# Six entries of the table of expected waits that merges the mixers' streams on TensorE: gates, softmax attention and token-major values later

## The chip, the cores and the metric

The kernel runs on one core of a Trainium2 chip. A core has a matrix engine (TensorE, "PE" in the profile), a vector engine (VectorE, "DVE"), an engine for activation functions (ScalarE, "ACT"), a general engine (GpSimd, "POOL") and an engine that issues DMAs (SyncE, "SP"). Each works through its own list of instructions in order; an instruction waits at the head of the list until what it needs is there, and all that stands behind it waits too. The metric is the device time of one execution in microseconds, the median of several runs.

## The reference, cut to what matters

One inference step of a two-layer trunk on 512 prompt positions and 8 x 4 sample positions, so 544 columns in all. In each layer four groups of "mixers" work on slices of one projection; their outputs are joined by `w_out`, and a gated feed-forward block with a short convolution follows.

```
def hybrid_layer(x, pos, k_pos, st, p):
    h = rmsnorm(x, p['norm1_g'])
    proj = h @ p['w_in']
    (a_qkv, a_z, a_b, a_a, b_b, b_c, b_h, c_q, c_k, c_v, d_u, d_v) = jnp.split(proj, ...)
    qkv, a_conv_new = causal_dwconv(st['a_conv'], a_qkv, p['a_conv_w'])
    q, k, v = l2norm(qkv[:, :, 0]), l2norm(qkv[:, :, 1]), qkv[:, :, 2]
    beta = jax.nn.sigmoid(a_b)
    g = -jnp.exp(p['a_log']) * jax.nn.softplus(a_a + p['a_dt_bias'])
    o, a_state_new = gated_delta_rule(q, k, v, g, beta, st['a_state'])      # group A
    ...
    out_b = b_b * bx                                                        # group B
    out_c = window_attn_banded(cq, ck, cv, p['c_sinks'])                    # group C
    out_d = chunk_token_mlp(du, dvn, p['d_ws'], p['d_bias'])                # group D
    x = x + jnp.concatenate([out_a, out_b, out_c, out_d], axis=-1) @ p['w_out']
    h2 = rmsnorm(x, p['norm2_g'])
    gate, f_conv_new = causal_dwconv(st['f_conv'], h2 @ p['ffn_w_gate'], p['ffn_conv_w'])
    return x + (jax.nn.silu(gate) * (h2 @ p['ffn_w_up'])) @ p['ffn_w_down'], new
```

## The kernel before, in words

Activations lie feature-major (128 features on the partitions, 544 positions along the free dimension). Each float32 product is made of three float32r products: high by high, high by low, low by high. So each weight tile is split in two: ScalarE copies the high part (`wh`, L734), VectorE subtracts it to get the low part (`wl`, L736).

In each layer a **main stream** (`main`) issues the large products in a fixed order: first the token-major projection (`ptm`), then 19 tiles of 128 output features (`pj_...`), of which the first nine are k0, q0, v0, cq0, cq1, ck, k1, q1, v1, then the output projection (`po1`, `po2`) and the feed-forward block (`pgt`, `pup`, `pA` to `pD`, `pdn`). A tile `pj_...` takes eight *steps*; a step is one slice of the contraction, 6 matmuls (two halves of 272 columns, three products each). Two PSUM buffers (`psmm`, pool `pmm`) hold the tiles in turn, so tile n+2 can begin only when VectorE has read tile n out. For k, q and v that reading is L1529 and L1530, for cq and ck it is L1550.

Beside it run **side streams**, one for each mixer and layer, written as Python generators:

- `gates` (g0 in layer 0, g1 in layer 1): the products `pg`, a chain of small VectorE instructions that ends in `gg` (L867), then the products `pe` on `gg`, read by `gcp` (L882) and `ex`.
- `mixer_a` (a00, a01, a10, a11: layer and pair of heads): norms (`pl`), decays (`pgb`, from `gg`), `pk` (k by k and k by q, in two halves that use the same PSUM buffer `pk`, so the second half waits until VectorE has read the first: `N` L967, `qk` L968), then `pkt`, k turned token-major, which VectorE makes into `kbe` and `kd` (L1006, L1008), then `pvt`, v turned token-major, in the same PSUM buffer as `pkt`, then a triangular inverse (`pW`, `pR`) and a scan (`p`).
- `decode_a` (e0, e1), `mix_d` (d0, d1), and `mix_c` (c0, c1): softmax attention in four blocks of scores (`psc`), transposes (`ptr`) and values (`pov`). The scores need `cq` and `ck` after their rotation, whose last VectorE instruction is L1555.

A class `Order` merges these streams into the one list of TensorE. It keeps a clock of its own in model microseconds, moved on by a price for each matmul. A stream yields either a delay or the name of an event; the table `LAT` adds, for a stream's n-th yield, a further delay. A side stream is taken as soon as its model time has come, otherwise the main stream goes on. TensorE's list is fixed in this way; the lists of the other engines are then made by a scheduler that works from the same program. The lines that use the table:

```
        w = LAT.get(st[3], {}).get(st[4], 0.0)
        if isinstance(y, tuple):
            st[0], st[2] = self.t, (y[1], w)
        else:
            st[0], st[2] = self.t + y + w, None
```

In `gates` the second yield is `yield 9.0`, between the chain to `gg` and the products `pe`. In `mix_c` the first is the wait for the event `c0` or `c1`, set 4.0 model us after the tile ck is issued. In `mixer_a` the twelfth is `yield 1.8`, between `pkt` and `pvt`.

Of the kernel before, what the change touches and what calls it, by code (L numbers as in the profile page):

```python
# [273 lines left out]
def _unhost(r):  # L274
# [8 lines left out]
    def conv(a, k, n):  # L283
# [19 lines left out]

LAT = {
    "a00": {
        3: 1.60, 13: 15.62, 14: 3.75, 15: 2.87, 16: 1.87, 17: 3.23, 18: 1.78, 19: 2.03, 34: 1.52,
    },
    "a01": {
        3: 3.96, 4: 1.12, 10: 2.64, 24: 0.84,
    },  # L310
    "a10": {
        3: 1.56, 13: 15.67, 14: 3.68, 15: 2.79, 16: 3.85, 17: 1.45, 25: 1.33, 36: 0.47, 42: 1.13,
    },
    "a11": {
        3: 3.59, 6: 3.32, 13: 1.06, 28: 0.70, 35: 0.30,
    },
    "c0": {
        1: 1.19, 2: 4.34, 5: 7.17, 6: 0.65, 7: 2.67, 8: 3.40,
    },
    "c1": {  # L320
        1: 0.81, 2: 4.06, 5: 7.68, 6: 0.61, 7: 15.38, 10: 1.48,
    },
    "d0": {
        4: 6.53,
# [5 lines left out]
        4: 3.69,  # L330
    },
    "g0": {
        2: 2.70,
    },
    "g1": {
        2: 2.53,
    },
}

# [1488 lines left out]
```

## Time and profile before

| | us |
|---|---|
| median of 3 runs | 1355.7 |
| lowest and highest run | 1353.25, 1356.69 |
| the profiled execution | 1355.9 |
| its span, first to last instruction | 1353.6 |
| TensorE busy | 1297.3 |
| VectorE busy | 994.2 |
| ScalarE busy | 638.2 |
| GpSimd busy | 459.6 |

The mixers of layer 0 take about the stretch from 35 to 260 us of the span, those of layer 1 from 699 to 925. A row of the timeline gives the start, the duration, the engine, the line, the operation, output and inputs, the count of instructions merged in the row, and in brackets the idle time of the engine just before with the instruction that ended it. All TensorE products have line L436 or L441, so they are told apart by their output. A row of the stretches gives from and to, the length, the busy time of TensorE, its weight loads, VectorE, ScalarE and GpSimd (with counts), TensorE's granted clock (1.00 is 2.4 GHz, 0.50 is 1.2 GHz), and two columns on DMA.

### The profile page before, as it was taken

How to read it: one execution, taken by the hardware profiler on the slowest of the kernel's cores; microseconds unless marked ns; L12 is line 12 of the kernel's file. 1: busy time of each engine (PE TensorE's matmuls, PEld its weight loads, DVE VectorE, ACT ScalarE, POOL GpSimd, SP SyncE). 2: the span in 40 equal slices, each digit the busy share in tenths (PEclk: the TensorE clock that was granted, in tenths of full speed). 3: DMA queues.
4: the chain of work that ended last, by engine and by line, in shares of the span. 5: the costliest groups of instructions: out<-in, count | busy, mean ns of one | idle time of the engine just before them, and what ended most of it. 6: DMA issues, size and time to landing. Idle time of an engine off the chain costs nothing.

```text
span 1353.6 us, 29982 instructions
## 1 busy us (share of the span) xinstructions
PE 1297.3 (96%) x12550; PEld 1247.8 (92%) x12550; DVE 994.2 (73%) x1579; ACT 638.2 (47%) x1116; POOL 459.6 (34%) x570
## 2 busy tenths in 40 slices
PE   9899999997999999999998999999979999999997
PEld 8888888996999999999998888889979999999997
DVE  6898944669689778777558977547697896886865
ACT  6436323454455445444434363335545554454453
POOL 2432320043365544542123322102334454643501
PEclk9899999997999999999998999999979999999999
DMA  7222241231233332333432221413212333232231
GB/s 277 82 66 81 79 131 42 87 100 33 79 99 96 104 93 87 104 93 103 157 104 81 77 84 53 137 40 95 98 31 79 110 98 91 94 108 87 87 100 67
DMA packets 48087, 125.61 MB, mean 93 GB/s; under 512 B 10144, under 2 KB 14432, under 8 KB 47824
## 3 DMA queue, kind: packets, MB, share of 16 engines
q1 hardware_dynamic: 47952, 123.70, 29.2%
q8 instruction: 98, 1.61, 0.5%
q14 instruction: 37, 0.30, 0.1%
HBM read 115.01 MB, written 8.67 MB: 91 GB/s over the span
## 4 chain that ended last, share of the span: by engine, by line
PE 79%; DVE 14%; ACT 3%; issue 3%; DMA 1%; DVEq 0%; SPq 0%; ACTq 0%
PE pdn L436 16%; PE pA L436 11%; PE pD L436 7%; PE po L436 7%; PE pB L436 4%; PE pup L436 4%; DVE wl L736 3%; PE pC L436 3%; PE pgt L436 3%; PE ptm L436 2%; PE pj_b L436 2%; PE pj_cq L436 2%; PE pj_z L436 2%; PE pj_h L436 2%; PE pj_c L436 2%
## 5 line engine op out<-in xcount | busy, mean ns | idle before, releaser
L736 DVE TENSOR_TENSOR wl<-wr,wh 128x768 fp32r<-128x768 f32 (+3 forms) x218 | 267.5, 1227 | 68.8 <-ACT wh L734 67.4
L734 ACT ACTIVATE wh<-wr 128x768 fp32r<-128x768 f32 (+3 forms) x218 | 193.1, 886 | 186.9 <-PE pA L436 32.8
L436 PE MATMUL pdn<-hdh,wh 128*128 128x272 f32 x680 | 141.5, 289 | 5.9 <-DVE up L1743 4.1
L436 PE MATMUL pdn<-hdl,wh 128*128 128x272 f32 x680 | 140.7, 288 | 0.5 <-DVE hdl L516 0.5
L436 PE MATMUL pdn<-hdh,wl 128*128 128x272 f32 x680 | 140.5, 288 | 0.0
L717 POOL TENSOR_TENSOR s<-wr 128x512 f32<-128x512 f32 x36 | 53.5, 1487 | 229.9 <-DMA wr<-w_u 140.8
L734 ACT ACTIVATE wh<-s 128x1024 fp32r<-128x1024 f32 x72 | 76.2, 1059 | 93.8 <-PE pdn L436 69.3
L436 PEld LDWEIGHTS pdn<-hdh,wh 128*128 128x128 f32 x680 | 106.5, 188 | 8.1 <-issue 3.9
L436 PEld LDWEIGHTS pdn<-hdl,wh 128*128 128x128 f32 x680 | 106.6, 188 | 0.9 <-DVE hdl L516 0.9
L736 DVE TENSOR_TENSOR wl<-s,wh 128x1024 fp32r<-128x1024 f32 x72 | 101.8, 1414 | 7.1 <-ACT wh L734 7.0
L436 PEld LDWEIGHTS pdn<-hdh,wl 128*128 128x128 f32 x680 | 106.5, 188 | 0.0
L798 DVE SCALAR_TENSOR_TENSOR cacc<-pbf,prm,cacc 128x560 f32<-128x560 f32 x88 | 78.6, 894 | 34.8 <-ACT cacc L796 34.0
L536 POOL TENSOR_TENSOR sq<-sq 128x544 f32<-128x544 f32 x18 | 30.8, 1715 | 201.3 <-DVE xl L562 135.3
L1769 DVE TENSOR_TENSOR xr<-xr,pdn 128x544 f32<-128x544 f32 x62 | 44.3, 715 | 47.2 <-PE pdn L436 47.1
L1669 POOL COPY sfo<-pbf 128x2 f32<-128x2 f32 x44 | 20.8, 472 | 136.7 <-DVE pbf L1734 84.0
L718 POOL TENSOR_TENSOR s<-wr,s 128x512 f32<-128x512 f32 x36 | 65.3, 1813 | 1.3
L720 POOL TENSOR_TENSOR s<-wr 128x512 f32<-128x512 f32 x36 | 62.1, 1725 | 0.0
L719 POOL TENSOR_TENSOR s<-wr,s 128x512 f32<-128x512 f32 x36 | 59.2, 1645 | 5.7 <-DVE wl L736 4.9
L796 ACT ACTIVATE cacc<-pbf,prm 128x560 f32<-128x560 f32 x44 | 33.6, 764 | 53.8 <-DVE pbf L1735 51.7
L516 DVE TENSOR_TENSOR hdl<-sl,hdh 128x544 fp32r<-128x544 f32 x44 | 41.3, 939 | 1.9 <-ACT hdh L515 1.8
L436 PE MATMUL pA<-f5h,wh 128*128 128x272 f32 x144 | 41.7, 289 | 0.0
L436 PE MATMUL pB<-f3h,wl 128*128 128x272 f32 x144 | 41.6, 289 | 0.0
(635 smaller groups left out, 4227.3 us busy)
## 6 DMA issues: line engine op xcount, KB each, us to landing
wr<-w_g SPq DMA_DIRECT2D x44, 512.0 KB
wr<-w_u SPq DMA_DIRECT2D x44, 512.0 KB
wr<-w_ch SPq DMA_DIRECT2D x38, 512.0 KB
wr<-w_d SPq DMA_DIRECT2D x48, 384.0 KB
wr<-w_o SPq DMA_DIRECT2D x12, 384.0 KB
wr<-w_d SPq DMA_DIRECT2D x16, 256.0 KB
xr<-x_in SPq DMA_DIRECT2D x7, 544.0 KB
wr<-w_tm SPq DMA_DIRECT2D x8, 392.0 KB
```

What stands on the lines that cost most here:

```text
L436: nc.tensor.matmul(out, lhsT, rhs, **kw)
L516: tt(lo, src, hi.bitcast(F32), op=ALU.subtract)
L536: (dve if self.last is not None else self.es[i]).tensor_tensor(self.acc[i], self.acc[i], sq, op=ALU.add)
L717: add(s12[:, lo_], u[:, lo_], u[:, hi_], op=ALU.add)
L718: add(s12[:, hi_], g[:, lo_], s12[:, lo_], op=ALU.add)
L719: add(s43[:, lo_], g[:, hi_], s12[:, hi_], op=ALU.add)
L720: add(s43[:, hi_], g[:, lo_], u[:, lo_], op=ALU.add)
L734: act(hi, r, AF.Copy)
L736: tt(lo, r, hi.bitcast(F32), op=ALU.subtract)
L796: act(acc[:, 0:out_n], pb[:, 0:out_n], AF.Copy, scale=wcol[:, 0:1])
L798: stt(acc[:, 0:out_n], pb[:, j:j + out_n], wcol[:, j:j + 1], acc[:, 0:out_n], op0=ALU.mult, op1=ALU.add)
L1769: tt(xk(m), xk(m), pflat(p), op=ALU.add)
```

## The change

Six numbers of the table are raised or added: the second yield of `gates` from 2.70 to 7.00 and from 2.53 to 6.80; the first of `mix_c` from 1.19 to 3.60 and from 0.81 to 3.20; and the twelfth of `mixer_a`'s first pair of heads, which had no entry, to 0.90 in both layers. No arithmetic changes. Lines of the diff:

```
     "a00": {
-        3: 1.60, 13: 15.62, 14: 3.75, 15: 2.87, 16: 1.87, 17: 3.23, 18: 1.78, 19: 2.03, 34: 1.52,
+        3: 1.60, 12: 0.90, 13: 15.62, 14: 3.75, 15: 2.87, 16: 1.87, 17: 3.23, 18: 1.78, 19: 2.03, 34: 1.52,
...
     "c0": {
-        1: 1.19, 2: 4.34, 5: 7.17, 6: 0.65, 7: 2.67, 8: 3.40,
+        1: 3.60, 2: 4.34, 5: 7.17, 6: 0.65, 7: 2.67, 8: 3.40,
...
     "g0": {
-        2: 2.70,
+        2: 7.00,
```

Since a side stream's time sets where it is merged, and the merged order sets the times of all that follows, the order changes through both mixer stages. In steps of the main stream, counted from the start of each layer's tiles, the side work stands as follows (layer 0): `pe` after step 20 before and 27 now, `pde` (the decode mixer's first products) 24 and 31, the first `pl` 35 and 34, `pgb` 45 and 44, `pk` 53 and 52, its second half 54 and 54, the first `psc` 54 and 56, `pkt` 56 and 56, `pvt` 59 and 60, then most groups one to three steps later. In layer 1: `pe` 20 and 26, `pk` 53 and 52, its second half 54 and 54, the first `psc` 54 and 55, `pkt` 56 and 55, `pvt` 59 and 59; from step 90 to 144 most groups of the second pair of heads and of the decode mixer stand one to six steps earlier than before.

TensorE, layer 0, at the gates (`pj_v` is the tile v0, `pj_cq` the tile cq0, `pe` the gates' second products), before:

```order
L436 MATMUL pj_v_631<-xh,wl 128x272 x2
L436 MATMUL pe<-gg,cst 128x16 x3
L436 MATMUL pe<-gg,cst 128x1 x2
L436 MATMUL pe<-gmk,cst 128x16
L436 MATMUL pj_v_631<-xh,wh 128x272 x2
```

and now:

```order
L436 MATMUL pj_cq_704<-xh,wl 128x272 x2
L436 MATMUL pe<-gg,cst 128x16 x3
L436 MATMUL pe<-gg,cst 128x1 x2
L436 MATMUL pe<-gmk,cst 128x16
L436 MATMUL pj_cq_704<-xh,wh 128x272 x2
```

The gates' products have moved from the middle of tile v0 to behind the third step of tile cq0.

TensorE, layer 0, at the first scores (a piece of the difference; `pj_k` is the tile k1, the `pk` row its second half, the first being two steps ahead):

```order
 L436 MATMUL pj_k_976<-xl,wh 128x272 x2
 L436 MATMUL pj_k_976<-xh,wl 128x272 x2
-L436 MATMUL psc<-ck,cq 128x128 x4
+L436 MATMUL pj_k_976<-xh,wh 128x272 x2
+L436 MATMUL pj_k_976<-xl,wh 128x272 x2
+L436 MATMUL pj_k_976<-xh,wl 128x272 x2
 L436 MATMUL pk<-kq_439 64x128 x8
 L436 MATMUL pj_k_976<-xh,wh 128x272 x2
```

The scores have left the place ahead of the second half of `pk`, and that half now comes two steps after the first with no scores between. VectorE's list at the same place, before:

```order
L736 TENSOR_TENSOR wl<-wr,wh 128x1024
L1553 TENSOR_TENSOR ck<-rp,rope 128x544
L1555 TENSOR_TENSOR ck<-ck,rs 128x544
L967 TENSOR_TENSOR N<-pk,N 128x256
L968 TENSOR_TENSOR qk<-pk,qk 128x256
```

and now:

```order
L1553 TENSOR_TENSOR ck<-rp,rope 128x544
L967 TENSOR_TENSOR N<-pk,N 128x256
L968 TENSOR_TENSOR qk<-pk,qk 128x256
L1555 TENSOR_TENSOR ck<-ck,rs 128x544
L967 TENSOR_TENSOR N<-pk,N 128x256
```

The reading of the first half of `pk` has moved ahead of the last instruction on `ck`.

VectorE, layer 1, at the token-major keys (`kbe`, `kd` from `pkt`; `pb` is the reading of tile k1, `wl` a weight split), before:

```order
L972 STREAM_TRANSPOSE NT<-N 128x512
L1240 TENSOR_SCALAR nm<-mx 128x4
L1529 TENSOR_TENSOR pb<-pj_k_9243,rstd 128x512
L1530 TENSOR_TENSOR pb<-pj_k_9243,rstd 128x8x4
L1242 TENSOR_TENSOR es<-prm_120,nm 128x4
L976 COPY_PREDICATED R<-cst,NT 128x256
L736 TENSOR_TENSOR wl<-wr,wh 128x1024
L1006 TENSOR_TENSOR kbe<-pkt,bec 128x512
L976 COPY_PREDICATED R<-cst,NT 128x256
L1008 TENSOR_TENSOR kd<-pkt,ex 128x512
```

and now:

```order
L972 STREAM_TRANSPOSE NT<-N 128x512
L1237 TENSOR_REDUCE mx<-sc 128x2
L1006 TENSOR_TENSOR kbe<-pkt,bec 128x512
L1008 TENSOR_TENSOR kd<-pkt,ex 128x512
L976 COPY_PREDICATED R<-cst,NT 128x256
L1238 TENSOR_TENSOR mx<-mx,prm_120 128x4
L1529 TENSOR_TENSOR pb<-pj_k_9243,rstd 128x512
L1530 TENSOR_TENSOR pb<-pj_k_9243,rstd 128x8x4
L736 TENSOR_TENSOR wl<-wr,wh 128x1024
```

`kbe` and `kd` have moved ahead of the reading of tile k1 and of a weight split.

## Rows read from the trace of the kernel before

**Rows 1.** The page: busy times, and the chain that ended last, by engine.

```profile
PE 1297.3 (96%) x12550; PEld 1247.8 (92%) x12550; DVE 994.2 (73%) x1579; ACT 638.2 (47%) x1116; POOL 459.6 (34%) x570
PE 79%; DVE 14%; ACT 3%; issue 3%; DMA 1%; DVEq 0%; SPq 0%; ACTq 0%
```

**Rows 2.** What TensorE waited for: total us, times, longest us.

```profile
PE pgt L436 <- DVE f1l L587: 16.1, 6, 6.0
PE pe L436 <- DVE gg L867: 8.7, 2, 4.3
PE psc L436 <- DVE ck L1555: 4.2, 2, 2.1
...
PE pvt L436 <- DVE kd L1008: 1.1, 2, 0.6
```

**Rows 3.** Stretches at the gates: length, busy PE PEld DVE ACT POOL, granted clock.

```profile
47.60:50.10 2.50, 0.00 (x1) 0.00 (x0) 2.47 (x8) 0.42 (x1) 0.36 (x1) 1.00 0.18 66
50.10:60.40 10.30, 8.46 (x39) 8.46 (x39) 6.76 (x18) 5.55 (x11) 2.60 (x6) 0.50 0.15 52
...
715.70:726.00 10.30, 8.69 (x40) 8.69 (x40) 6.67 (x18) 5.33 (x9) 2.60 (x6) 0.50 0.15 52
```

**Rows 4.** Timeline of TensorE, layer 0: start, duration, instruction, idle before.

```profile
44.42 0.41 PE L436 MATMUL pj_v<-xh,wh 128*128 128x272 f32 x2
...
47.19 0.41 PE L436 MATMUL pj_v<-xh,wl 128*128 128x272 f32 x2
51.94 2.29 PE L436 MATMUL pe<-gg,cst 128*128 128x16 f32 x10 [4.34 <-DVE gg L867]
...
54.52 0.80 PE L436 MATMUL pj_v<-xh,wh 128*128 128x272 f32 x2
...
60.83 0.50 PE L436 MATMUL pj_cq<-xh,wh 128*128 128x272 f32 x2
...
88.59 0.72 PE L436 MATMUL psc<-ck,cq 64*128 64x128 f32 x8 [2.10 <-DVE ck L1555]
...
96.23 1.15 PE L436 MATMUL pvt<-cst,vt 64*64 64x64 f32 x32 [0.54 <-DVE kd L1008]
```

**Rows 5.** Timeline of VectorE, layer 0.

```profile
51.38 0.18 DVE L1530 TENSOR_TENSOR pb<-pj_q,rstd 128x32 f32<-128x32 f32 x1
...
60.35 0.69 DVE L1529 TENSOR_TENSOR pb<-pj_v,rstd 128x512 f32<-128x512 f32 x1 [3.42 <-PE pj_v L436]
...
86.94 1.60 DVE L1555 TENSOR_TENSOR ck<-ck,rs 128x544 f32<-128x544 f32 x1
...
88.80 0.41 DVE L968 TENSOR_TENSOR qk<-pk,qk 128x256 f32<-128x256 f32 x1
...
95.41 0.68 DVE L1008 TENSOR_TENSOR kd<-pkt,ex 128x512 f32<-128x512 f32 x1
```

**Rows 6.** Stretches from the changed VectorE order to `qk` and `kd`.

```profile
55.10:89.20 34.10, 32.00 (x241) 31.12 (x240) 28.68 (x43) 14.58 (x25) 13.89 (x12) 0.92 0.28 92
720.30:754.70 34.40, 32.29 (x242) 31.37 (x241) 28.70 (x43) 14.58 (x25) 13.81 (x12) 0.92 0.27 93
55.10:96.10 41.00, 38.46 (x319) 36.88 (x318) 35.40 (x61) 18.72 (x37) 15.56 (x16) 0.94 0.26 80
```

**Rows 7.** Timeline of TensorE, layer 1, at the same three places.

```profile
717.31 2.29 PE L436 MATMUL pe<-gg,cst 128*128 128x16 f32 x10 [4.31 <-DVE gg L867]
...
754.06 0.72 PE L436 MATMUL psc<-ck,cq 64*128 64x128 f32 x8 [2.11 <-DVE ck L1555]
...
761.70 1.15 PE L436 MATMUL pvt<-cst,vt 64*64 64x64 f32 x32 [0.55 <-DVE kd L1008]
```

**Rows 8.** Other waits of TensorE, and the clock after the first of them.

```profile
311.30 0.39 PE L436 MATMUL pgt<-f1l,wh 128*128 128x272 f32 x1 [1.71 <-DVE f1l L587]
...
788.30 0.75 PE L436 MATMUL pR<-Wc,Tm 32*32 32x32 f32 x64 [1.39 <-ACT Wc L1024]
...
313.00:330.00 17.00, 9.21 (x36) 8.29 (x36) 17.00 (x24) 7.35 (x15) 7.38 (x8) 0.50 0.00 0
```

## What was predicted

> **What bounds the kernel now.** First the page: TensorE is busy for 1297 of 1354 us and holds 79% of the chain that ended last, VectorE 14% [rows 1]. So time is won only where TensorE stands idle or runs at a lower clock. Second the list of what it waited for [rows 2]. The largest entry, 16.1 us for `f1l` at the start of the feed-forward block, is not touched. The next ones in the mixers are those of the three raised entries: `gg` 8.7, `ck` 4.2 and `kd` 1.1 us, each twice, once a layer. Third the stretches around the gates [rows 3]: TensorE does nothing from 47.6, VectorE is busy for 2.47 of the 2.50 us up to 50.1, and then the granted clock stands at 0.50 for 10.3 us, though TensorE is busy for 8.46 of them. So the wait for `gg` costs twice, once as idle time and once as half speed after it. Layer 1 repeats it with 8.69 busy us. Fourth, VectorE's own rows: between 55.1 and 89.2 it is busy for 28.68 of 34.1 us [rows 6], and its largest idle time, 3.42 us, is a wait for tile v0, which the half clock made late [rows 5]. VectorE is close to its limit there. That decides how much of the gain survives.
>
> **What the change takes away.** (1) The gates' wait. `pe` goes behind the rest of v0 and some steps of cq0, so TensorE has work while VectorE finishes `gg`. This removes 4.34 us in layer 0 [rows 4] and 4.31 in layer 1 [rows 7]. (2) The half clock after it. 8.46 and 8.69 us of work at 0.50 would take half at 1.00: 4.2 and 4.3 us [rows 3]. (3) The waits for `ck`, 2.10 and 2.11, and for `kd`, 0.54 and 0.55 [rows 4, 7]. Together 8.54 + 8.5 + 4.21 + 1.09 = 22.3 us. Nothing is added to any engine's work; the instructions are the same.
>
> **What comes late next: the buffer of tile q0.** Tile cq0 uses the PSUM buffer that q0 leaves when L1530 has read it, at 51.38 + 0.18 = 51.56 [rows 5]. A step takes 0.755 us (12 pairs start 0.252 apart, 44.42 to 47.19 [rows 4]), so v0's last four steps end at 47.60 + 3.02 = 50.6, and cq0 waits for about 0.95 us. The L1530 of layer 1 stands at the same distance from `gg`, so 1.9 us in both. The nearest rows are waits of 1.39 and 1.71 us; a clock fall follows the second and not the first [rows 8]. I take no fall.
>
> **What comes late next: the second half of `pk`.** From cq0's start to the old wait for `ck` TensorE needs 60.83 to 86.49, or 25.7 us, and now also `pe` (51.94 to 54.52 at half clock, so 1.3) and the three `pde` products, some 0.6 by the six of `pe` [rows 4]. So it comes to that half at 51.6 + 25.7 + 1.9 = 79.2. There it must wait until VectorE has read the first half (L968). VectorE's list up to L968 holds the same instructions as before except that L1555 on `ck`, 1.60 us, now comes after it. With no idle time at all it ends at 55.1 + 28.68 - 1.60 = 82.2 [rows 5, 6]. So TensorE waits for 3.0 us at a place where it waited for `ck` for 2.1; L968's old end, 89.21, shows that this half was already as late as the scores ahead of it. In layer 1 the same sum gives 720.3 + 28.70 - 1.60 = 747.4 for VectorE; TensorE, idle from 713.0, is there the same 31.6 us later as in layer 0 (47.6 to 79.2), at about 744.6, so it waits for 2.8. The entry for the scores only lets them give their place to another reader of the same queue.
>
> **Then `kd`.** VectorE ends `kd` at 55.1 + 35.40 = 90.5 at the earliest [rows 6]. TensorE has 7.25 us of work from the second half of `pk` to `pvt` (the half itself about 1.0 and `pkt` 1.1, by the 1.15 of `pvt`; six steps 4.5; the scores 0.65), so at full clock it arrives at 89.45 and waits for about 1.1. `pvt` begins near 90.6 where it began at 96.23, and one step more of the main stream lies before it: a gain of 5.6 + 0.75 = 6.4 us. In layer 1 `kd` stands some 2.9 us earlier in VectorE's list, and there are five steps, not six, so `pvt` follows at 747.4 + 6.5 = 753.9 against 761.70: 7.8 us. From `pvt` on I carry these gains through: what follows keeps its distances or is one to three steps later in layer 0, and in the stretch after the mixers TensorE is the only busy engine. For the groups of layer 1 that come up to six steps earlier I take nothing; their bounds are the wait of 1.39 us there, which may go, and about two new ones of that size [rows 8].
>
> **Does the clock fall again?** This is the open price. A wait of 2.1 us brought no fall, 4.3 us brought one, and so did 1.71 us amid full-width products [rows 3, 4, 8]. The new wait of 3.0 us lies between, nearer to the cases that fell in kind: it is one unbroken gap, with half-filled products around it. I take a fall as the likelier. It would begin about 2.5 us into the gap, as at the gates (47.6 to 50.1), and last 10.3 us, to about 92.0. TensorE then does 4.9 of its 7.25 us of work by 92.0 and begins `pvt` at 94.35: a gain of 1.9 + 0.75 = 2.6 us. In layer 1 it lasts to 757.3, 4.95 of 6.5 us are done, and `pvt` begins at 758.9: 2.8 us. The Trainium skill, "TensorE: Matmul & The Clock Gate", section "HAM oscillation — how this bites in real kernels", says that a loop whose matrix engine waits between its bursts falls back to the half clock at every such wait, and its section "Terms" prices a fall at half of the time for which it holds. By that rule filling one gap only moves the fall to the next, and of the 8.5 us in (2) nothing would stay; the trace agrees as to the price and, by the wait of 2.1 us without a fall, not as to every wait.
>
> **The sum.** Against the profiled execution's 1355.9 us (span 1353.6 and 2.3 around it; the median is 1355.7, so nothing is shifted): 2.6 + 2.8 = 5.4 us, **1350.5 us**.
>
> **The rivals.**
> - *The new wait brings no fall.* For it: waits of 2.1 us are free of one; VectorE's instructions may be slower or faster by a microsecond. Gain 6.4 + 7.8 = 14.2: 1341.7. With a fall in one layer only, 9.2 to 10.4: about 1346.
> - *All three waits go and VectorE does not bind.* It would need VectorE to end L968 3 us sooner than its own busy time allows. Gain 22.3 - 1.9 = 20.4: 1335.5. Small chance.
> - *Nothing is won.* The fall at `pk` holds for 17 us, as after 311.3 [rows 8], and costs 3.4 us more in each layer: 5.4 - 6.8 = -1.4, so 1357.3, no change that can be told.
> - *Slower.* In layer 1 the second pair of heads and the decode mixer come one to six steps earlier, so TensorE reaches products whose inputs ScalarE or VectorE has not made; two waits of 1.7 us, each with a fall of 4.2, cost 11.8: 1350.5 + 11.8 = 1362.3. It decides from about 9.5 us of such losses. Against it: the rows show one wait of 1.39 us in that stretch, and VectorE is less busy there.
> - *The table doesn't move what it says.* Excluded: the order shows `pe` behind three steps of cq0.
>
> **How the numbers follow.** Fall in both layers 0.42, in one 0.2, in none 0.18, all waits gone 0.05, nothing won 0.09, slower 0.06. The likeliest is the first, with a range of its own from 1348.5 to 1352.5, since the unknown is where in the gap the fall begins. The range for 8 in 10 goes from 1340 to 1354.5: it leaves out the case with all waits gone, the lower part of "none", and the last two cases above. A difference of 0.3% is 4.1 us, about what a measurement of this kernel can tell from no change; the limit is 1351.6. Of the first case some seven tenths lie below it, all of the next three but a little: 0.29 + 0.19 + 0.18 + 0.05 = 0.71 faster, 0.23 within, 0.06 slower.
>
> **What would show it.** In the changed kernel's list of TensorE's waits `gg`, and `ck` ahead of `psc`, should be gone or under 0.5 us each; an entry for `pk` released by `qk` (L968) of about 3 us a layer should be new; one for `pj_cq` released by L1530, about 1 us. The stretch that held clock 0.50 at the gates should read 1.00, with a new stretch of 0.50 some 30 us later. VectorE should show almost no idle time from 55 to 90 us. I am wrong if `pk` waits for under 1.5 us, if VectorE's busy time in that stretch changes by more than 2 us, or if a new wait appears after `pvt`.

## The result, and the profile after

The changed kernel takes 1364.4 us (six runs, 1361.25 to 1368.76) where the kernel before takes 1355.5 beside it: a ratio of 1.007, with a 95% interval from 1.0049 to 1.0092. It became slower by 0.7%. The prediction was 1350.5 with a range of 1340 to 1354.5, so it is wrong in sign. The profiled execution took 1367.5 us, 3 above the median; its span is 1365.7, 12.1 more than before.

The page after, its busy times and its chain [rows 1]: TensorE's work is the same, its share of the chain fell from 79 to 74%, and what came in is "issue" and ScalarE.

```profile
PE 1300.5 (95%) x12550; PEld 1248.7 (91%) x12550; DVE 992.8 (73%) x1579; ACT 637.4 (47%) x1115; POOL 458.0 (34%) x570
PE 74%; DVE 14%; issue 5%; ACT 5%; POOL 1%; DMA 1%; SPq 0%; DVEq 0%; ACTq 0%; POOLq 0%
```

TensorE's timeline of layer 0 up to `pvt`, only rows with a wait or of the gates (it answers to [rows 4]):

```profile
51.12 0.49 PE L436 MATMUL pj_cq<-xh,wh 128*128 128x272 f32 x2 [1.09 <-DVE d L865]
53.46 1.17 PE L436 MATMUL pe<-gg,cst 128*128 128x16 f32 x10
...
62.05 0.43 PE L436 MATMUL pl<-sqd,cst 128*128 128x64 f32 x2 [1.15 <-ACT ex L884]
67.53 0.50 PE L436 MATMUL pl<-hvh,bonesr 128*128 128x512 f32 x1 [1.98 <-ACT sqd L922]
84.75 1.09 PE L436 MATMUL pk<-kq 64*64 64x128 f32 x16 [0.77 <-DVE qk L968]
93.81 1.15 PE L436 MATMUL pvt<-cst,vt 64*64 64x64 f32 x32 [1.32 <-DVE mx L1238]
```

The waits for `gg` and `ck` are gone. The first row is the wait for q0's buffer (L865 is the neighbour of L1530 in VectorE's list). Two waits are new and were not in the prediction's sum: `pl` waits for ScalarE, for `ex` and `sqd`. `pvt` starts 2.4 us earlier in the span than before, 1.8 us earlier when counted from the start of v0. The same place in layer 1, which answers to [rows 7]:

```profile
733.75 0.43 PE L436 MATMUL pl<-sqd,cst 128*128 128x64 f32 x2 [1.04 <-ACT ex L884]
739.23 0.50 PE L436 MATMUL pl<-hvh,bonesr 128*128 128x512 f32 x1 [1.97 <-ACT sqd L922]
756.43 1.09 PE L436 MATMUL pk<-kq 64*64 64x128 f32 x16 [2.26 <-DVE qk L968]
763.34 1.15 PE L436 MATMUL pvt<-cst,vt 64*64 64x64 f32 x32
```

What comes behind `pvt`, in the rows of TensorE's waits and of its timeline (layer 0 at 126.71, the rest layer 1):

```profile
126.71 1.07 PE L436 MATMUL pR<-Wc,Tm 32*32 32x32 f32 x64 [5.59 <-ACT Wc L1024]
...
793.52 1.15 PE L441 MATMUL ptr<-cst,sc 128*128 128x128 f32 x8 [2.56 <-DVE sc L1253]
803.58 0.42 PE L436 MATMUL pmd<-wm,dvd 32*64 32x32 f32 x4 [2.76 <-ACT oc L1354]
840.38 1.05 PE L441 MATMUL ptr<-cst,sc 128*128 128x128 f32 x4 [1.72 <-DVE vnd L1211]
870.16 0.32 PE L436 MATMUL pR<-Wc,Tm 32*32 32x32 f32 x14 [1.26 <-issue]
```

And the stretches with their granted clock (columns as in [rows 3]):

```profile
47.00:50.50 3.50, 3.04 (x25) 2.81 (x23) 3.47 (x9) 1.41 (x3) 1.07 (x2) 1.00 0.22 83
50.50:60.80 10.30, 9.68 (x78) 9.59 (x78) 10.11 (x20) 6.34 (x11) 4.82 (x9) 1.00 0.31 99
69.08:72.49 3.41, 3.41 (x16) 3.22 (x15) 3.41 (x6) 2.95 (x4) 0.68 (x1) 0.50 0.10 20
123.69:130.52 6.83, 3.81 (x77) 3.75 (x78) 3.70 (x12) 3.05 (x9) 0.00 (x0) 0.50 0.01 2
802.95:809.77 6.82, 6.19 (x105) 5.39 (x105) 3.65 (x7) 1.23 (x3) 1.55 (x3) 0.50 0.02 7
```

The gates run at full clock now. The half clock stands at other places, three of them behind waits: at 69 behind `pl`, at 124 in the wait of `pR`, at 803 in that of `pmd`. Two shorter ones, 3.4 us each, follow the waits at 840 and 870.

**Where the time went.** The main stream is the same in all these kernels, so the start of one and the same step can be compared. Steps are counted here through both layers: layer 1 starts with step 152. The table gives it against the kernel before, in us, set to zero at the start of v0 in layer 0; each column is one profiled execution. Side work that stands earlier or later shifts a single row by one or two us. The experiments of the other columns follow below.

| step, and its start before | after | gates alone (e1) | gates at 24 (e5) | rear kept (e6) | rear kept in layer 1 (e13) | e9 |
|---|---|---|---|---|---|---|
| 32, behind `pe` and `pde`, 66.9 | -7.1 | -7.1 | -7.1 | -7.1 | -7.1 | -6.9 |
| 48, ahead of `pk`, 80.6 | -1.9 | -1.9 | -4.6 | -1.9 | -3.5 | -4.6 |
| 60, behind `pvt`, 98.2 | -2.7 | -1.9 | -4.9 | -1.8 | -1.3 | -4.9 |
| 148, end of layer 0's mixers, 224.2 | +5.5 | -1.4 | -4.7 | +2.4 | +6.9 | -4.8 |
| 168, v0 of layer 1, 709.8 | +6.5 | -1.0 | -4.5 | +0.3 | +8.4 | -5.8 |
| 184, behind the gates, 732.4 | -0.8 | -8.2 | -9.9 | -7.0 | +1.2 | -11.3 |
| 212, behind `pvt`, 763.6 | +2.2 | -1.6 | -8.0 | -4.0 | +4.2 | -13.0 |
| 303, end of layer 1's tiles, 895.7 | +14.3 | -0.2 | -8.2 | -3.4 | +6.8 | -12.7 |

Read the first column downwards: 7.1 us won at the gates, 5.2 of them given back before `pk`, 2.7 left behind `pvt`. From there to the end of the mixers layer 0 loses 8.2. Layer 1 wins 7.3 at its gates, has 4.3 left behind `pvt`, and then loses 12.1.

### The profile page after: what moved, and what is told of

Same layout as the page of the kernel before. It is cut to its first block, busy times and chain, and to the rows that moved or that the text cites. A ratio compares the mean times of both kernels' runs of the same rounds, so it can differ in the third digit from the quotient of the medians.

```text
span 1365.7 us, 29991 instructions
## 1 busy us (share of the span) xinstructions
PE 1300.5 (95%) x12550; PEld 1248.7 (91%) x12550; DVE 992.8 (73%) x1579; ACT 637.4 (47%) x1115; POOL 458.0 (34%) x570
## 4 chain that ended last, share of the span: by engine, by line
PE 74%; DVE 14%; issue 5%; ACT 5%; POOL 1%; DMA 1%; SPq 0%; DVEq 0%; ACTq 0%; POOLq 0%
PE pdn L436 16%; PE pA L436 11%; PE pD L436 7%; PE po L436 7%; PE pB L436 4%; PE pup L436 4%; PE pgt L436 3%; PE pC L436 3%; DVE wl L736 3%; PE pj_z L436 2%; PE ptm L436 2%; PE pj_b L436 2%; DVE cacc L798 2%; PE pj_h L436 2%; PE pj_c L436 2%
## 5 line engine op out<-in xcount | busy, mean ns | idle before, releaser
L736 DVE TENSOR_TENSOR wl<-wr,wh 128x768 fp32r<-128x768 f32 (+3 forms) x218 | 272.2, 1249 | 70.8 <-ACT wh L734 69.6
L717 POOL TENSOR_TENSOR s<-wr 128x512 f32<-128x512 f32 x36 | 56.9, 1581 | 229.6 <-DMA wr<-w_u 107.3
L798 DVE SCALAR_TENSOR_TENSOR cacc<-pbf,prm,cacc 128x560 f32<-128x560 f32 x88 | 78.8, 896 | 34.4 <-ACT cacc L796 33.5
L720 POOL TENSOR_TENSOR s<-wr 128x512 f32<-128x512 f32 x36 | 62.1, 1724 | 0.0
L436 PE MATMUL pD<-f4h,wl 128*128 128x272 f32 x144 | 41.6, 289 | 0.0
```

What stands on the lines that cost most here:

```text
L436: nc.tensor.matmul(out, lhsT, rhs, **kw)
L717: add(s12[:, lo_], u[:, lo_], u[:, hi_], op=ALU.add)
L720: add(s43[:, hi_], g[:, lo_], u[:, lo_], op=ALU.add)
L736: tt(lo, r, hi.bitcast(F32), op=ALU.subtract)
L798: stt(acc[:, 0:out_n], pb[:, j:j + out_n], wcol[:, j:j + 1], acc[:, 0:out_n], op0=ALU.mult, op1=ALU.add)
```

## The experiments

Theory A: what the change wins ahead of `pvt` is real, and it is the order behind `pvt` that makes it slower. Rival B: the moves ahead of `pvt` themselves cost, through VectorE or through later falls of the clock. All ratios are against the kernel before, run beside.

**e1 to e3: one entry at a time.**

```
e1   "g0": { 2: 7.00 },  "g1": { 2: 6.80 }
e2   "c0": { 1: 3.60, ... },  "c1": { 1: 3.20, ... }
e3   "a00", "a10": { ..., 12: 0.90, ... }
```

> Only the gates' entries are raised (7.00 and 6.80); scores and values keep their old entries. TensorE's list behind pvt is then that of the kernel before, to the step. Theory A (the gates' gain is real, and the loss of the changed kernel comes from where scores and values then stand in the lists behind pvt): both waits for gg go and the half clock after them, and of the 17 us about 3 us a layer are kept up to pvt and carried on, since nothing behind pvt moves: about 1349, certainly under 1352. Rival B (VectorE and later falls of the clock take back all that the gates win, and this is why the changed kernel is slower): 1355 or more.

Measured: 1352.9 us, 0.9975 [0.9966, 0.9985]. This lies between the two forecasts.

> Only the entries of the scores are raised (3.60 and 3.20). The waits for gg and the half clock after them stay. TensorE's list of layer 1 behind pvt is nearly that of the changed kernel, that of layer 0 is a third one (fourth block of scores and second pk at step 112 where they stood at 100). Theory A: layer 1 loses the 7 us that it loses in the changed kernel, with at most 4 us of ck's waits won: 1356 to 1364. Rival B (the gates' move is the cause): 1352 to 1355, the waits for ck being won and nothing lost.

Measured: 1377.9 us, 1.016 [1.014, 1.018]. This is beyond both, 21.7 us slower than before. From `pvt` to the end of the mixers its trace loses 12 us in each layer.

> Only the entries of the values are added (0.90 in both layers). pvt moves by one step, and with it the merge behind it: the last pk and scores of layer 0 come one to two steps earlier, those of layer 1 up to 15 steps earlier. The largest wait that can go is kd's 1.1 us. Theory A: whatever it does is done behind pvt, 1353 to 1360. Rival B: within 1 us of before, 1354.5 to 1356.5.

Measured: 1356.7 us, 0.9998 [0.9989, 1.0007]. The time does not separate A from B. The trace shows two changes that cancel: layer 0 loses 5.8 us up to v0 of layer 1, and layer 1 wins 3.0.

So the gates' move is good by 3.3 us and keeps the order behind `pvt`; it is not the cause. The scores' entries are the largest part, but e2 moves the scores and the order behind them together, so it does not say which of the two costs. The three do not add (-3.3 + 21.7 + 0.5 is 18.9, all together give 8.9), since each changes the merge for the others. That speaks against B as far as the gates go. For e1, A's figure of 1349 was too good: 7.1 us won at the gates shrink to 1.9.

**e4 and e12: one layer at a time.** All three entries in layer 0, or in layer 1.

> All three entries raised in layer 0, none in layer 1, whose list is that of the kernel before. The trace of the changed kernel is 5.3 us late at the start of the feed-forward block of layer 0, and of its 12 us the other 7 arise in layer 1. If the layers do not interact: 1355.5 + 5.3 = 1360.8, with the wait of 5.6 us of pR for ScalarE's Wc and the clock at 0.50 around 124 to 130 us. If the loss of layer 1 is only an echo of layer 0 (weights or transfers that come late): 1364 or more.

Measured: 1362.5 us, 1.0047 [1.0034, 1.0060], between the two figures and nearer to the first; `pR` waits for `Wc` for 5.3 us.

> All three entries raised in layer 1, none in layer 0. If the layers' losses add: 1364.4 + 1355.6 - 1362.5 = 1357.5. If layer 1 loses by itself what its stretch of the profiled execution shows (8 us from the start of the tiles to the end of the mixers): 1363.

Measured: 1358.0 us, 1.0013 [1.0000, 1.0026]. The layers add: 0.47 and 0.13% make 0.60, within the interval of the changed kernel. Its trace loses 6.1 us between v0 of layer 1 and the end of the tiles, but wins back 3.8 behind them; at the start of the feed-forward block the half clock lasted for 10.2 us there and not 17.1.

**e5: the gates earlier, right behind v0.**

```
-    "g0": { 2: 2.70 },  "g1": { 2: 2.53 }
+    "g0": { 2: 5.20 },  "g1": { 2: 5.00 }
```

> Only the gates' entries are raised, and to 5.20 and 5.00: pe comes right behind tile v0 (step 24 where the first run of gates alone has 27), all groups behind it stand as there. With pe behind three steps of cq0 the exponential ex of ScalarE came at 62.0 where it was at 56.0, De at 66.2 where it was at 62.4, and pl waited for them for 1.1 and 2.0 us a layer, with a clock fall of 3.4 us. Theory A (ScalarE's list behind pe takes back the gates' gain, so an earlier pe keeps more of it): pe at about 51.7, those two waits under 1.5 us together, no fall at 69: 1349 to 1351. Rival B (VectorE's busy time up to ck decides, ScalarE does not matter): the wait for ck grows by what the others lose, 1352.3 to 1353.5 as with gates alone.

Measured: 1348.0 us, 0.9944 [0.9931, 0.9957], 1 us below A's range. Its TensorE, layer 0 (this execution began 1.8 us later than that of e1):

```profile
53.39 1.27 PE L436 MATMUL pe<-gg,cst 128*128 128x16 f32 x10 [1.29 <-DVE gg L867]
...
68.43 0.50 PE L436 MATMUL pl<-hvh,bonesr 128*128 128x512 f32 x1 [1.99 <-ACT sqd L922]
85.33 0.72 PE L436 MATMUL psc<-ck,cq 64*128 64x128 f32 x8 [1.96 <-DVE ck L1555]
92.86 1.15 PE L436 MATMUL pvt<-cst,vt 64*64 64x64 f32 x32 [0.54 <-DVE kd L1008]
```

`pe` takes the place of the wait for q0's buffer, and the wait for `ex` is gone. The wait for `sqd` stays in layer 0, against the expectation, and falls to 0.3 us in layer 1. No fall follows at 69, but that says little: e4, e7 and e13 have the changed kernel's list there, with `pe` at 27, and show none at 69 either. What counts is VectorE. In e1 it waits for ScalarE at `De` (first row below); in e5 it does not (third row):

```profile
66.47 0.19 DVE L1138 TENSOR_TENSOR De<-De,cst 128x32 f32<-128x32 f32 x1 [2.87 <-ACT De L1137]
84.43 0.42 DVE L968 TENSOR_TENSOR qk<-pk,qk 128x256 f32<-128x256 f32 x1 [0.84 <-POOL qk L957]
...
65.22 0.18 DVE L1138 TENSOR_TENSOR De<-De,cst 128x32 f32<-128x32 f32 x1
83.26 0.42 DVE L968 TENSOR_TENSOR qk<-pk,qk 128x256 f32<-128x256 f32 x1 [0.85 <-POOL qk L957]
```

Counted from the start of v0 in layer 0 (44.14 in e1, 45.91 in e5), L968 ends after 40.7 us in e1 and 37.8 in e5. It is 40.7 to 40.8 in all runs with `pe` at 27 there, with or without a half clock at 69, and 37.8 in all three with `pe` at 24. Between v0's start and that end VectorE is idle for 4.0 us in e1 and 1.8 in e5, and busy for 36.7 and 36.0. So most of the 2.9 us is VectorE waiting for ScalarE: that is A.

**e6 and e8: the front moved, the order behind `pvt` put back.**

```
e6   "c0": { 1: 3.60, 2: 1.93, ... },  "c1": { 1: 3.20, 2: 2.30, ... },  "a10": { ..., 12: 0.40, ... },  gates 7.00, 6.80
e8   the same, gates 5.20, 5.00
```

> Gates and scores raised as in the changed kernel, in both layers, but what the scores' entry adds is taken from their next one (4.34 to 1.93, 4.06 to 2.30), and in layer 1 the values get 0.40: so the first scores stand behind the second half of pk as in the changed kernel, and every group behind pvt stands at its step of the kernel before. Theory A (the loss lies in the order behind pvt, not in the moves ahead of it): under 1354, at best 1349, with no wait of pR for Wc above 2 us and none of pmd for oc. Rival B (moving the scores behind the second half of pk is itself what costs): 1360 or more.

Measured: 1354.0 us, 0.9988 [0.9977, 1.0000], at the upper edge of A's range. `pR` waits for `Wc` for 0.4 us at most, and `pmd` not for `oc`, as A said.

> As the run with the rear kept, with the gates' entries at 5.20 and 5.00 (pe at step 24). If the places of pe and of the scores act separately, this is that run's time plus the difference between gates at 24 and gates at 27. Theory A: the best of all, 1347 to 1350. Rival B: no better than gates alone, 1352 or more.

Measured: 1349.0 us, 0.9948 [0.9933, 0.9962], in A's range, though e5 is no slower.

With the rear kept, nearly the same front costs nothing: 10.4 us less than the changed kernel. That is A. It is not free in layer 0, though. There the first softmax starts later while its readers stay, and three new waits appear (e6):

```profile
93.92 1.15 PE L436 MATMUL pvt<-cst,vt 64*64 64x64 f32 x32 [2.08 <-DVE mx L1238]
101.41 0.92 PE L441 MATMUL ptr<-cst,sc 128*128 128x128 f32 x4 [0.87 <-DVE sc L1253]
105.41 0.92 PE L436 MATMUL pov<-pt,cv 128*64 128x256 f32 x4 [1.57 <-ACT pt L1346]
```

So in layer 0 the scores have no better place in either form; in layer 1 they have. The run e9 below shows both by times: it differs from e8 in layer 0's scores alone and is 5.1 us faster, and from e5 in layer 1's scores and values alone and is 4.1 us faster. B is therefore right in part: in layer 0 the scores' new place costs 5.1 us with the gates at 24, even with the rear kept.

**e10: the scores undone.** The changed kernel with 1.19 and 0.81 put back.

> The changed kernel with the scores' entries put back (1.19 and 0.81); gates and values stay raised. The merge behind pvt is then that of the run with the values alone, which lost 5.8 us in layer 0 and won 3.0 in layer 1. Theory A (what the front wins and what the new rear order costs simply add, by layer): 1356.7 of that run less the 3.3 that gates alone won, about 1353.4. Rival B (the gates' move and the values' move disturb each other): 1357 or more.

Measured: 1354.6 us, 0.9989 [0.9979, 0.9998], 1.2 above A's figure and below B's. The scores' two entries are 9.8 us of the changed kernel's time. But layer 0 is not cured: in this trace it still is 8.2 us late at v0 of layer 1, by other waits (`ptr` waits 2.85 us for `vbd` at 147, with a half clock of 6.8 us beside it), and e3, with the same order behind `pvt`, shows the same wait. What this trace wins, 3.9 us, it wins in layer 1.

**e13: the changed kernel with layer 1's rear put back** (`"c1"` 2: 2.30, `"a10"` 12: 0.40).

> The changed kernel with two more numbers in layer 1: the scores' second entry at 2.30 (4.06) and the values' at 0.40 (0.90). Everything that the change moves ahead of pvt stays moved, in both layers; layer 0 is the changed kernel's throughout; in layer 1 every group behind pvt is back at its step of the kernel before. Theory A (in layer 1 the loss is the order of the second pair of heads, the decode mixer and the later scores, up to 12 steps earlier than before): the waits of ptr for sc, pmd for oc and ptr for vnd in layer 1 go, with the falls of the clock behind them; layer 1 wins the 3.6 us that it won in the run with both rears kept, and layer 0 loses 6: 1357 to 1359.5. Rival B (layer 1 loses because it starts 6 us later or because of the scores' new place ahead of pvt): 1362 or more.

Measured: 1360.1 us, 1.0030 [1.0019, 1.0042], 4.2 less than the changed kernel and a little above the expected range. In the trace layer 1 goes from a loss of 7.8 to a gain of 1.6, more than the times show; the waits that stood at 793, 803 and 840 and the falls behind them are gone (one fall of 3.4 us stands at 884). Nothing ahead of `pvt` in layer 1 was changed but `pvt`'s own entry. So in layer 1 it is the order behind `pvt`. For layer 0 the same step is the one from e13 to e6: they have the same order of TensorE in layer 1 and, in layer 0, up to `pvt`, which stands at 60 in e13 and at 59 in e6; all behind it is at the old steps in e6 and one to three later in e13. The times are 1360.1 and 1354.0, so layer 0's rear costs 6.1 us. The two steps, 4.2 and 6.1, make up the 10.4 between the changed kernel and e6.

**e7: the copy that `pR` waits for, on another engine.** Which wait of the new order makes layer 0 lose? ScalarE's list ahead of the late `Wc`, after (start, duration, instruction, idle before). `hvh` is the high part of the squares of k1 and q1 that GpSimd makes (`sql`), `vt` the silu of v1, `sc` the exp of the second block of scores, `du` the gelu of u0, `es` a small exp that ends the same softmax:

```profile
117.31 0.63 ACT L895 ACTIVATE hvh<-sql 128x512 fp32r<-128x512 f32 x1 [4.87 <-POOL sql L916]
...
118.79 0.61 ACT L1534 ACTIVATE vt<-cacc 128x512 f32<-128x512 f32 x1
...
120.83 0.51 ACT L1246 ACTIVATE sc<-sc,nm 128x256 f32<-128x256 f32 x1 [1.30 <-DVE wl L736]
...
122.92 1.28 ACT L1585 ACT_TABLE_LOAD   x1
124.21 0.66 ACT L1585 ACTIVATE du<-du 128x544 f32<-128x544 f32 x1
126.18 0.20 ACT L1248 ACTIVATE es<-es 128x4 f32<-128x4 f32 x1 [1.31 <-issue]
126.29 0.36 ACT L1024 ACTIVATE Wc<-pW 128x256 f32<-128x256 f32 x1
```

and before:

```profile
113.52 0.51 ACT L1246 ACTIVATE sc<-sc,nm 128x256 f32<-128x256 f32 x1 [1.31 <-DVE wl L736]
...
115.50 0.61 ACT L895 ACTIVATE hvh<-sql 128x512 fp32r<-128x512 f32 x1
116.02 0.19 ACT L1248 ACTIVATE es<-es 128x4 f32<-128x4 f32 x1
...
120.54 0.66 ACT L1585 ACTIVATE du<-du 128x544 f32<-128x544 f32 x1
121.10 0.36 ACT L1024 ACTIVATE Wc<-pW 128x256 f32<-128x256 f32 x1
```

Before, the second block's exp goes first, then `es`, `vt`, `du` and `Wc`. After, exp stands behind `hvh` and `vt`, and `es` behind `du`. ScalarE switches its function table three times between the silu of q1 and `Wc` in both (1.3 us each), but after the change all three come behind `hvh` and `vt`, the last of them at `es`.

```
-            act(Wc, pW, AF.Copy)
+            dve.tensor_copy(Wc, pW) if (l, pr, s) == (0, 0, 4) else act(Wc, pW, AF.Copy)
```

> The changed kernel with one copy moved from ScalarE to VectorE: the first Wc of layer 0 (L1024), which TensorE waits 5.6 us for. No other instruction changes its place on any engine; in VectorE's list the copy stands behind the weight split that ends at 120.6. Theory A (ScalarE's list, with exp of the scores, two table loads, du and es ahead of Wc, costs 5.6 us of waiting and half of a 6.8 us fall): pR starts near 121.5, and 9 us come back: about 1355.5. Rival B (the same exp, es, holds VectorE's list as well: the reading of pR, L1030, stands behind a VectorE instruction that waits for es until 126.4): pR comes at 121.5, but the next pW waits for about 4 us, and the time stays within 2 us of the changed kernel's 1364.4.

Measured: 1363.6 us, 1.0060 [1.0046, 1.0074]. `pR` comes at 121.4 as both expected, and then:

```profile
121.43 0.75 PE L436 MATMUL pR<-Wc,Tm 32*32 32x32 f32 x64
127.86 1.94 PE L441 MATMUL ptr<-cst,sc 128*128 128x128 f32 x8 [4.73 <-DVE sc L1253]
```

This is B's result by B's cause, one place on: not the next `pW` but the transposes of the same scores wait, since VectorE stands for 4.73 us at the same `es`. The copy was the first victim of the late softmax, not the cause.

**e11: SyncE's queue.** `hvh` waits for GpSimd, GpSimd for the load of `wmt`. In SyncE's list of the changed kernel the store `o_sao` now stands ahead of that load:

```profile
107.19 0.41 SPq L1367 DMA_DIRECT2D dbias<-dbias  x1
110.80 0.34 SPq L1575 DMA_DIRECT2D o_sao<-sao  x1
111.19 0.43 SPq L1361 DMA_DIRECT2D wmt<-wmt  x1
```

```
-            nc.sync.dma_start(O["sao"][l], sao)
+            (nc.scalar if l == 0 else nc.sync).dma_start(O["sao"][l], sao)
```

> The changed kernel with one store of layer 0 (o_sao, L1575) issued from ScalarE's queue and not from SyncE's. No other instruction changes its place on any engine. In SyncE's list this store stands ahead of the load of wmt in the changed kernel (behind it before), and waits for GpSimd's copy at 110.8, so wmt is issued at 111.19 where it was issued at 105.55; GpSimd's second sql, ScalarE's hvh, the exp of the scores and Wc follow. Theory A (this crossing in SyncE's list is the root of what layer 0 loses): wmt is issued near 107.7, exp of the scores starts near 117.8 and not 120.8 (then VectorE's nm holds it), Wc 3 us earlier, pR's wait 2.6 and not 5.6, and 3 us come back, 6 if no fall of the clock follows: 1358 to 1361.5. Rival B (the scores' own later place holds exp): within 1 us of 1364.4.

Measured: 1364.9 us, 1.0062 [1.0047, 1.0078]. `wmt` is issued at 107.45, `hvh` runs at 113.82 and not 117.31, all as A says, and exp still starts at 120.25. VectorE has become the late one. Its step of the convolution (`cacc`) is held up, ScalarE's silu `vt` waits for that, and exp stands behind `vt` and a table switch:

```profile
110.91 4.49 DVE L798 SCALAR_TENSOR_TENSOR cacc<-pb,prm,cacc 128x568 f32<-128x568 f32 x1
...
118.19 0.63 ACT L1534 ACTIVATE vt<-cacc 128x512 f32<-128x512 f32 x1 [2.35 <-DVE cacc L798]
...
120.25 0.51 ACT L1246 ACTIVATE sc<-sc,nm 128x256 f32<-128x256 f32 x1 [1.30 <-DVE es L1242]
```

The crossing in SyncE's queue is real and not what decides. Two links of the chain were removed one at a time, each did what was expected of it, and neither gave a microsecond: at least two are late together. Which of them, or whether the second block's own place (three steps later) suffices, stays open for layer 0. Shown is that 6.1 us of it go when layer 0's rear is put back (e13 to e6). Putting back the scores' entries alone does not do it: that order loses in layer 0 by other waits (e10).

**e9: the better half of each layer.** Gates at 24 in both; layer 0 as in e5, layer 1 as in e8.

> Gates at step 24 in both layers (5.20, 5.00); scores raised in layer 1 only, with the rear kept (first entry 3.20, next one 2.30, values 0.40); layer 0 has the scores of the kernel before. In the traces of the earlier runs, from the start of v0 to the end of the mixers, layer 0 won 4.7 us with gates alone at 24 and 0.6 with the scores moved as well, and layer 1 won 3.7 and 6.6. If the layers add: 1355.6 - 4.7 - 6.6 = 1344.3, faster than the 1348.0 of gates alone at 24. If what the scores win in layer 1 was only the clock's luck of one execution: 1347 to 1349.

Measured: 1343.9 us, 0.9912 [0.9897, 0.9927]: 12.3 us faster than before and 20.5 faster than the change. The layers add: the sum, 1344.3, is 0.4 us off.

## Why the prediction was wrong, point by point

- *What is removed.* Right. `gg` and `ck` are off the list of waits, the gates run at clock 1.00, and 7.1 us are won by step 32 where the terms gave 4.3 + 4.2 less 0.95, or 7.55. Most of the difference is the price of the half clock: in v0 the pairs of matmuls start 0.453 us apart at 0.50 (55.12 to 59.65) against 0.252 at 1.00, a factor of 1.8 and not 2, so the 8.46 us were worth 3.8 and not 4.2.
- *q0's buffer, 0.95 us.* Right: 1.09 and 1.02.
- *`pk`, 3.0 and 2.8 us.* Mis-sized: 0.77 and 2.26; in e4, e7 and e13, which have the same list there and no half clock at 69, layer 0 has 2.3. The sum let VectorE run "with no idle time at all" and gave ScalarE no time. Its end of L968, 82.2, is 37.8 us after the start of v0 (44.42). That is what e5, e8 and e9 show, with `pe` at 24 (in part by luck, since VectorE is idle for 1.8 us there); the changed kernel shows 40.8. For `ex` and `De` hang on `pe` and `pde`. With `pe` behind three steps of cq0, ScalarE's list has a copy that waits for GpSimd (`hvh`) ahead of `ex`, and the silu of v0 with its table load ahead of `De`. So VectorE stood for 2.88 us at `De`, and `pl` waited 1.15 + 1.98 us: TensorE came to the second half of `pk` at 83.98 where the sum had 79.2.
- *A fall at `pk` in both layers.* Wrong in the profiled execution: none in either layer, at waits of 0.77 and 2.26. One of 3.41 us came at 69, behind the wait of 1.98. In e13 one of 3.41 us does stand at `pk` in layer 0 (at 85.2, in the wait of 2.27), a third of the length forecast; e4 and e7 have the same wait and no fall.
- *Gain up to `pvt`, 2.6 + 2.8.* 2.7 + 4.3 measured. The size was right in layer 0 by other terms than those of the sum, which is luck.
- *"From `pvt` on I carry these gains through."* **This step failed.** The order listing showed groups one to three steps later in layer 0 and mostly one to six earlier in layer 1 (a few stand nine earlier), and the sum priced that at nothing. It cost 8.2 and 12.1 us in the profiled execution, which is 3 us above the median (e7 and e11, with the same list, lost 6.8 and 13.1 there in layer 1); by times, 6.1 us in layer 0 (e13 to e6) and 4.2 in layer 1 (the changed kernel to e13). These two pairs of runs show that it is the order behind `pvt`. Through which wait is shown less well. The moved groups were not counted on the engines that feed them: in layer 0 ScalarE's exp, `du` and `es` changed places, and a store went ahead of a load on SyncE's queue; in layer 1 `ptr` and `pmd` came ahead of what they read. In layer 0 removing one such link at a time won nothing (e7, e11), so the chain there stays open. One reason given for the step was also misread: behind the mixers TensorE is not the only busy engine; from 340 to 700 us VectorE is busy for 261.9 of 360 us.
- *The signs of being wrong.* Two of the three came: `pk` waits for under 1.5 us in layer 0, and new waits stand behind `pvt`.
- *The rival "slower", 1362.3.* It named the mechanism, for layer 1, and its time is 2.1 us off, in part by luck: its base and its losses are not those measured. It had a chance of 0.06 for the reason that the rows before show one wait of 1.39 there. That was the wrong evidence: the waits of the old order say little of a new one. And it left layer 0 out, which by e4 and e12 loses more than layer 1 (6.4 and 1.8 us).

The prediction cited the Trainium skill, "TensorE: Matmul & The Clock Gate", section "HAM oscillation — how this bites in real kernels", for falls at every wait between bursts. That section of the Trainium skill tells of a loop whose waits, some 3 to 5 us by its drawing, are longer than these; for single waits of 2 us the traces after do not bear out such a rule: there was no fall behind 2.26 us, one behind 1.98 in layer 0, and none behind 1.97 in layer 1 of the same execution.

## What to carry to other kernels

Where a merge or a scheduler rebuilds every engine's list from a few numbers, a gain at one place is safe only as far as the order behind it stays: compare the lists behind the edit on every engine, DMA queues too, and count a changed rear as a cost of its own, or put it back with the next entry. The edit that keeps the rear (the gates') won; the same front with a changed rear lost. A product that waits may be better moved into the next existing gap (`pe` into the wait for q0's buffer, 1348.0 us) than as far as its wait is long (1352.9 us), since others hang on its result. And a late reader behind a chain of in-order lists need not be cured at one link: here two attempts won less than 1 us.

## What the runs showed of the hardware

- **A VectorE instruction that waits for GpSimd's.** `cacc` (L798, two inputs in SBUF) took 4.49 us in e11 at 110.91. GpSimd worked from 110.22 to 114.78 without a gap of note. In that trace the 67 rows of this line with no GpSimd work beside them took 0.81 us at most, and all that took over 0.85 had some. The Trainium skill, "SBUF — State Buffer", section "SBUF: two separate sides", says that a VectorE instruction with two SBUF inputs and a GpSimd instruction that reads SBUF exclude each other, each for the whole instruction. The row fits that, and shows that one VectorE instruction can wait for four GpSimd instructions in a row; the profile shows the wait as a longer instruction, not as idle time.
- **One list, several times.** e7 and the changed kernel have the same TensorE list. In layer 1 one lost 2.6 us from the tiles' start to their end and the other 7.9, for the most part by where the clock fell. The half clock at the start of layer 1's feed-forward block lasted 17.1 us in ten of the fifteen traces, 13.7 in e2 and e7, and 10.2 in e1, e6 and e12, with the same work. A loss read from one trace is that uncertain.
- **One wait, with a fall and without.** In layer 0 the changed kernel, e4, e7, e11 and e13 have the same TensorE list up to `pvt`, and `pl` waits there for 1.15 us and then 1.97 or 1.98. A half clock of 3.4 us follows at 69 in the changed kernel and e11, and none there in the other three. It moved the second half of `pk` in none of them: that began 40.9 us after the start of v0 in all five, when VectorE was ready.
